# A hybrid encoder layer on one core: opening loads in order, side loads one unit ahead, up factors in every product

## The chip, the cores and the metric

One NeuronCore of a Trainium2 chip. TensorE multiplies, VectorE, ScalarE and GpSimd do elementwise work, and DMA queues that SyncE (SP) and GpSimd feed bring data from HBM to SBUF and back. The metric is the device time of one execution in microseconds. Before the change it is 2768.53 us (median of 3 runs, 2767.21 to 2771.9).

## The reference

Everything is float32; 1024 tokens, 2048 channels.

```python
mod = silu(c) @ w_ada + b_ada;  shift, scale, gate = split(mod, 3)       # w_ada: 2048 x 6144
h = rms_norm(x, g_pre) * (1 + scale) + shift
q, f, i, z, bb, cc, vb, zb = split(h @ w_in, 8)                          # w_in: 2048 x 8192
y_a = rms_norm(hgrn2(q, log f, 1 - f, i)) * silu(z)                      # 8 heads, chunks of 64 tokens
y_b = bb * causal_conv3(cc * vb) * silu(zb)
m_a, m_b = split(sigmoid(h @ w_merge + b_merge), 2)                      # w_merge: 2048 x 4096
out = (m_a * (y_a @ w_up_a) + m_b * (y_b @ w_up_b)) @ w_o                # w_up: 1024 x 2048 each
x = x + gate * rms_norm(out, g_post)
```

## The kernel before, in words

**The products.** Each large product is cut into 2x2 blocks and done with seven block products in place of eight (Strassen's scheme in Winograd's form); the stages are called p1, p6, p2, p7, p5, p4 and p3. A factor is a sum of blocks. Each float32 operand is split into a high part and a rest (`split_w` for weights, tiles w_hi and w_lo; `split_h` for activations, tiles called fp or yp), and one block product is three matmuls: hi x hi, hi x rest, rest x hi (`mm3`, L118). ScalarE casts the high part, VectorE subtracts to get the rest. A product of a unit has 24 matmuls of 128x512 (8 groups g of 3).

**The opening (L301 to L313).** x is loaded in 16 tiles, normed, and transposed on TensorE into xT. `ada_pair(q)` (L228) computes a quarter of shift and scale: 16 loads of w_ada (`ada_load`, L218; 512 KB each); the scale row is summed by TensorE into prow (L235), the shift row by VectorE into row_v, one multiply-add per load half (L239). Eight small matmuls pa (L244) turn the rows into columns a_c and sh_c. After the next pair `factors_a` makes from them the activations of two groups g and their factors for p1, p6, p2 and p7, which stay in SBUF. The scheduler orders the DMA issues on SP by its own simulated time line unless `keep_in_program_order` pins them.

**Phase 1 (L404).** 48 units: 32 of w_in (a head's or a convolution tile's two column blocks) and 16 of w_merge. `unit_a(u)` (L329) loads four weight blocks into a ring of five "raw" buffers, makes the sums s1, s2 and s4 and the difference in a21 on VectorE, and does p1, p6, p2 and p7. The sums and partial results are written to DRAM. Side work hangs on the units: `factors_b` makes the factors for p5, p4 and p3 (u below 16), `gate_step` sums the gate row of w_ada (u from 16), `sums_o` makes the block sums of w_o (u from 32). Side loads go into the shared pool `big` of 38 slots of 512 KB, and are issued with the sums that use them.

**Phase 2 (L682).** For each unit p5, p4 and p3, with the recurrence and the convolution as side steps in a list `later`. From unit 33 on, when `later` is empty, a step of `y_factors` (L634) makes the factors yp of the up-projections from the branch results y, and writes them to yf_scr in DRAM.

**The up-projections (`up`, L724).** First branch B, then A: 28 loads of 512 KB bring the factors yp back from yf_scr, then 8 units of seven products with 12 matmuls each. Gates g are loaded by GpSimd into `big` slots. After that comes the output product with w_o.

**What sets the order.** The order on each engine is fixed when the kernel is built, by the scheduler's simulated time line; a tile that is to reuse a slot waits for the slot's last reader.

Of the kernel before, what the change touches and what calls it, by code (L numbers as in the profile page):

```python
# [26 lines left out]
def tile_hgrn2_shortconv_block(  # L27
# [145 lines left out]
    ph = ph_pool.__enter__()  # L173
    xrow = [[None] * 2 for _ in range(8)]
# [26 lines left out]
    def transpose_x(hf):  # L201
        for k in range(KT):
# [6 lines left out]
            if k % 2:  # L209
# [46 lines left out]
    def factors_a(gs, vec=()):  # L256
# [26 lines left out]
        for g, b11, b12, b21, b22 in parts:  # L283
            keep_f("p7", g, b12)
# [15 lines left out]

    for si in range(8):  # L301
# [18 lines left out]
    units = [(w_in_v, (2 * j) * 1024 + i * P, (2 * j + 1) * 1024 + i * P) for i in range(NH) for j in range(4)]  # L320
    units += [(w_merge_v, 256 * m, 256 * m + P) for m in range(16)]

    def load_q(view, par, e0):
        raw = wp.tile([P, 8, P], F32, tag="raw", name="w_raw", bufs=5)
        nc.sync.dma_start(out=raw, in_=view[:, par, :, e0:e0 + P])
        return raw

    def unit_a(u):
        view, e1, e2 = units[u]  # L329
        a11, a21 = load_q(view, 0, e1), load_q(view, 0, e2)  # L330
        a22, a12 = load_q(view, 1, e2), load_q(view, 1, e1)
        o = ph.tile([P, 3, HS], F32, tag="o", name="o", bufs=2)
        s1, s2, s4 = (ph.tile([P, 8, P], F32, tag=f"s{n}", name=f"s{n}") for n in (1, 2, 4))
        px, py = ps("mm", "px"), ps("mm", "py")
        w1 = split_w(a11)
        if u:
            product(px, w1, fa["p1"])
        nc.vector.tensor_add(out=s1, in0=a21, in1=a22)
        nc.vector.tensor_sub(out=s2, in0=s1, in1=a11)
        nc.gpsimd.dma_start(out=s_scr[u][:, 0], in_=s1.rearrange("p a b -> p (a b)"))  # L340
        w6 = split_w(s2)
        if u == 0:
            for gs in (range(6), (6, 7)):
                product(px, w1, fa["p1"], pin=True, gs=gs)
                product(py, w6, fa["p6"], pin=True, gs=gs)
        nc.scalar.copy(out=o[:, 2], in_=px)
        if u:
            product(py, w6, fa["p6"])
        nc.vector.tensor_add(out=o[:, 1], in0=o[:, 2], in1=py)
        nc.vector.tensor_sub(out=s4, in0=a12, in1=s2)  # L350
        nc.gpsimd.dma_start(out=s_scr[u][:, 1], in_=s4.rearrange("p a b -> p (a b)"))
        product(px, split_w(a12), fa["p2"], more=True)
        nc.scalar.copy(out=o[:, 0], in_=px)
        nc.vector.tensor_sub(out=a21, in0=a11, in1=a21)
        product(py, split_w(a21), fa["p7"], more=True)
        nc.vector.tensor_add(out=o[:, 2], in0=o[:, 2], in1=py)
        nc.gpsimd.dma_start(out=u_scr[u], in_=o)
# [280 lines left out]
    def y_factors(br, g):  # L638
# [17 lines left out]
    side = [f for g in range(4) for br in (1, 0) for f in y_factors(br, g)]  # L656
# [37 lines left out]
    for n, (u, s) in enumerate(seq):  # L694
# [15 lines left out]
        elif u >= 33 and side:  # L710
# [273 lines left out]
```

## Time and profile before

| what | value |
|---|---|
| median of 3 runs | 2768.53 us (2767.21 to 2771.9) |
| profiled execution | 2769.2 us, span 2767.5 us |
| mean granted TensorE clock | 0.984 |
| TensorE busy | 2673.0 us (97%) |
| VectorE busy | 1716.7 us (62%) |
| ScalarE busy | 906.3 us (33%) |
| GpSimd busy | 280.0 us (10%) |
| DMA traffic | 631.30 MB, mean 228 GB/s |
| first product of unit 0 starts | 142.04 us |
| first product of phase 2 starts | 1213.65 us |
| first product of the up-projections starts | 2108.78 us |

The busy time of TensorE is modelled from the starts of pipelined matmuls, so that 97% is the share of time in which one was under way, at whatever clock. The clock stands beside it as the granted share of full speed. The time of the profiled execution exceeds its span by 1.7 us, which lie before and behind it.

### The profile page before, as it was taken

What the parts mean: (1) busy time and instruction counts of PE and PEld (TensorE: products, weight loads), DVE (VectorE), ACT (ScalarE), POOL (GpSimd) and SP (SyncE); (2) the same over time, 40 slices, a digit from 0 to 9 for tenths busy, and PEclk for the clock granted to TensorE, in tenths of its full rate; (3) what the DMA queues carried; (4) which work ended last, traced back from release to release, by engine and by line L of the source; (5) the groups of instructions that cost most, each with busy time, mean ns of one, the idle gap of its engine ahead of it and who ended that gap; (6) DMA issues with size and microseconds to landing.
All of it is one profiled execution on the core that took longest, in us unless ns stands there. A gap on an engine that the chain in (4) does not pass through costs nothing.

```text
span 2767.5 us, 31307 instructions
## 1 busy us (share of the span) xinstructions
PE 2673.0 (97%) x11851; PEld 2152.7 (78%) x11851; DVE 1716.7 (62%) x2096; ACT 906.3 (33%) x1176; POOL 280.0 (10%) x495
## 2 busy tenths in 40 slices
PE   4889999999999999999999999999998999999997
PEld 3267878888888888888888888888885787888786
DVE  6777886754554444546666666656563666765667
ACT  4433222222222222233344444435442222232333
POOL 2012111110000000010000000002111101100000
PEclk9899999999999999999999999999998999999999
DMA  9769999985556655584444444359999569773353
GB/s 361 286 201 313 345 349 364 346 292 179 179 192 179 182 175 177 174 316 137 133 130 133 138 146 138 110 178 374 360 363 407 187 213 335 235 282 99 99 178 142
DMA packets 420071, 631.30 MB, mean 228 GB/s; under 512 B 19564, under 2 KB 281808, under 8 KB 419792
## 3 DMA queue, kind: packets, MB, share of 16 engines
q1 hardware_dynamic: 358528, 394.31, 44.7%
q0 software_dynamic: 60208, 230.78, 21.7%
q10 hardware_dynamic: 1184, 4.20, 0.4%
q8 instruction: 93, 1.52, 0.2%
q14 instruction: 58, 0.48, 0.0%
HBM read 431.04 MB, written 198.18 MB: 227 GB/s over the span
## 4 chain that ended last, share of the span: by engine, by line
PE 81%; issue 8%; DMA 7%; DVE 2%; POOL 1%; ACT 1%; DVEq 0%; POOLq 0%; ACTq 0%; SPq 0%
PE po L866 10%; PE pz L119 7%; PE pz L122 7%; PE pz L123 7%; PE px L119 6%; PE px L123 6%; PE px L122 6%; PE py L123 6%; PE py L119 6%; PE py L122 6%; PE pw L119 4%; PE pw L122 4%; PE pw L123 4%; DMA yp<-yf_scr 3%; DMA ga_raw<-in_w_ada_dram 2%
## 5 line engine op out<-in xcount | busy, mean ns | idle before, releaser
L130 ACT CAST w_hi<-w_raw 128x1024 fp32r<-128x1024 f32 (+1 forms) x296 | 290.9, 983 | 1001.6 <-PE px L122 402.5
L131 DVE TENSOR_TENSOR w_lo<-w_raw,w_hi 128x1024 fp32r<-128x1024 f32 (+1 forms) x296 | 335.7, 1134 | 273.1 <-ACT w_hi L130 263.4
L123 PE MATMUL py<-fp,w_lo 128*128 128x512 f32 x768 | 301.2, 392 | 6.9 <-DVE w_lo L131 6.9
L123 PE MATMUL px<-fp,w_lo 128*128 128x512 f32 x768 | 300.9, 392 | 5.2 <-DVE w_lo L131 5.2
L119 PE MATMUL px<-fp,w_hi 128*128 128x512 f32 x768 | 301.2, 392 | 0.0
L122 PE MATMUL py<-fp,w_hi 128*128 128x512 f32 x768 | 299.5, 390 | 1.3 <-DVE fp L136 1.3
L119 PE MATMUL py<-fp,w_hi 128*128 128x512 f32 x768 | 299.8, 390 | 0.9 <-ACT w_hi L130 0.9
L122 PE MATMUL px<-fp,w_hi 128*128 128x512 f32 x768 | 300.0, 391 | 0.0
L866 PE MATMUL po<-w_hi,lt 128*128 128x512 f32 x896 | 244.2, 390 | 0.6 <-DVE og L900 0.6
L866 PEld LDWEIGHTS po<-w_hi,lt 128*128 128x128 f32 x896 | 168.1, 188 | 37.2 <-DVE og L900 2.2
L130 ACT CAST w_hi<-s 128x512 fp32r<-128x512 f32 (+1 forms) x112 | 90.1, 805 | 285.9 <-PE py L122 245.5
L123 PEld LDWEIGHTS py<-fp,w_lo 128*128 128x128 f32 x768 | 144.5, 188 | 41.5 <-DVE w_lo L131 11.2
L123 PEld LDWEIGHTS px<-fp,w_lo 128*128 128x128 f32 x768 | 144.8, 188 | 36.9 <-DVE w_lo L131 6.5
L122 PEld LDWEIGHTS py<-fp,w_hi 128*128 128x128 f32 x768 | 144.5, 188 | 32.1 <-DVE fp L136 1.7
L122 PEld LDWEIGHTS px<-fp,w_hi 128*128 128x128 f32 x768 | 145.1, 189 | 30.8 <-issue 0.5
L119 PEld LDWEIGHTS px<-fp,w_hi 128*128 128x128 f32 x768 | 144.9, 189 | 30.8 <-issue 0.7
L119 PEld LDWEIGHTS py<-fp,w_hi 128*128 128x128 f32 x768 | 144.5, 188 | 30.8 <-ACT w_hi L130 1.3
L119 PE MATMUL pz<-fp,hi 128*128 128x512 f32 x384 | 152.5, 397 | 3.0 <-DVE d L701 3.0
L122 PE MATMUL pw<-fp,w_hi 128*128 128x512 f32 x384 | 150.8, 393 | 0.0
L119 PE MATMUL pz<-fp,w_hi 128*128 128x512 f32 x384 | 150.5, 392 | 0.0
L123 PE MATMUL pz<-fp,lo 128*128 128x512 f32 x384 | 150.4, 392 | 0.0
L119 PE MATMUL pw<-fp,w_hi 128*128 128x512 f32 x384 | 150.4, 392 | 0.0
(286 smaller groups left out, 4959.4 us busy)
## 6 DMA issues: line engine op xcount, KB each, us to landing
w_raw<-in_w_in_dram SPq DMA_DIRECT2D x160, 512.0 KB, 5.2
s_scr<-s POOLq DMA_DIRECT2D x96, 512.0 KB, 6.0
s_raw<-s_scr SPq DMA_DIRECT2D x96, 512.0 KB, 4.3
w_raw<-in_w_merge_dram SPq DMA_DIRECT2D x80, 512.0 KB, 5.7
u_scr<-o POOLq DMA_DIRECT2D x48, 768.0 KB, 7.5
ada_raw<-in_w_ada_dram SPq DMA_DIRECT2D x64, 512.0 KB, 10.8
yf_scr<-yp POOLq DMA_DIRECT2D x56, 512.0 KB, 9.0
yp<-yf_scr SPq DMA_DIRECT2D x56, 512.0 KB, 12.8
```

The costliest lines, as they stand in the source:

```text
L119: mm = nc.tensor.matmul(o, ah, bh, start=first, stop=False, skip_group_check=True)
L122: nc.tensor.matmul(o, ah, bl, start=False, stop=False, skip_group_check=True)
L123: nc.tensor.matmul(o, al, bh, start=False, stop=last, skip_group_check=True)
L130: nc.scalar.copy(out=hi, in_=raw)
L131: nc.vector.tensor_sub(out=lo, in0=raw, in1=hi.bitcast(F32))
L866: nc.tensor.matmul(o, a, b[:, c], start=st, stop=sp, skip_group_check=True)
```

## The change

Six things are changed.

1. The loads of x, w_ada and the first two units' weights are pinned in program order on SP (`load`). The program puts unit 0's weights ahead of the last pair of rows. In the first three pairs all w_ada tiles lie in `big`. Small tiles move (`rows` into the raw ring, `row_p` into o0), and fewer copies of the second half's transposes go to VectorE.
2. Unit 0 is a generator: its splits and sums stand before the last pair of rows, its products behind the last factors, and it runs p1, p6 and p2 over the groups 0 to 5 first and 6 and 7 after, then p7.
3. `factors_b` is issued after the last sum of units 2, 4, ... 16. From unit 2 on the block a11 has buffers of its own (`ph`).
4. The loads of `gate_step` and `sums_o` are issued one unit ahead of the sums, pinned, from unit 10 and unit 26 on.
5. The steps of `y_factors` run first for branch A and then for B, one in every product from unit 33 on, and B's p1 factors stay in SBUF and are neither written nor read back.
6. The gates g of the up-projections have a ring of four; the pb loads are pinned.

The diff, without the parts that only move code of `unit_a`:

```diff
+    def load(o, i):
+        tc.keep_in_program_order(nc.sync.dma_start(out=o, in_=i))
...
-            nc.sync.dma_start(out=t, in_=x[si * P:(si + 1) * P, q * S:(q + 1) * S])
+            load(t, x[si * P:(si + 1) * P, q * S:(q + 1) * S])
...
-            if k % 2:
+            if k % 2 and (hf == 0 or k % 4 == 1):
                 nc.vector.tensor_copy(out=xT[k][:, halves[hf]], in_=p)
...
-        if n_ada[0] % 3:
+        if q < 3 or n_ada[0] % 4:
             raw = bigt(F32, "ada_raw").rearrange("p (k e) -> p k e", k=2)
         else:
-            raw = ph.tile([P, 2, HS], F32, tag="ada", name="ada_raw", bufs=4)
-        nc.sync.dma_start(out=raw, in_=w_ada_v[:, k:k + 2, t, q * HS:(q + 1) * HS])
+            raw = ph.tile([P, 2, HS], F32, tag="ada", name="ada_raw", bufs=2)
+        load(raw, w_ada_v[:, k:k + 2, t, q * HS:(q + 1) * HS])
...
+    def load_a(u):
+        view, e1, e2 = units[u]
+        if u > 1:
+            a11 = ph.tile([P, 8, P], F32, tag="a11", name="a11")
+            nc.sync.dma_start(out=a11, in_=view[:, 0, :, e1:e1 + P])
+        else:
+            a11 = load_q(view, 0, e1, pin=True)
+        return [a11] + [load_q(view, *a, pin=u < 2) for a in ((0, e2), (1, e2), (1, e1))]
...
+        if u == 0:
+            v.tensor_sub(out=a21, in0=a11, in1=a21)
+            w2 = split_w(a12, out_t=(ph.tile([P, 8, P], F32R, name="hi3a", bufs=1), wp.tile([P, 8, P], F32R, tag="raw", name="lo3a", bufs=5)))
+            yield
+            p2 = ps("mm", "p2")
+            for gs in (range(6), (6, 7)):
+                for p, w, f in ((px, w1, "p1"), (py, w6, "p6"), (p2, w2, "p2")):
+                    product(p, w, fa[f], pin=True, gs=gs)
...
     for q in range(1, 4):
+        if q == 3:
+            first = unit_a(0, load_a(0))
+            next(first)
         ada_pair(q)
         factors_a((2 * q - 2, 2 * q - 1))
-    factors_a((6, 7), vec=(7,))
+    with tc.issue_after(factors_a((6, 7), vec=(7,)).ins):
+        next(first, None)
...
     def gate_step(n):
...
-        nc.sync.dma_start(out=raw, in_=w_ada_v[:, 2 * kq:2 * kq + 2, 2, eb * HS:(eb + 1) * HS])
+        load(raw, w_ada_v[:, 2 * kq:2 * kq + 2, 2, eb * HS:(eb + 1) * HS])
+        yield
...
+    side = []
     for u in range(NU):
-        unit_a(u)
-        if u < 16:
-            if u % 2 == 0:
-                factors_b(u // 2)
-        elif u < 32:
-            gate_step(2 * u - 32)
-            gate_step(2 * u - 31)
-        elif u % 2 == 0:
-            sums_o((u - 32) // 2)
+        if u:
+            for _ in unit_a(u, load_a(u)):
+                pass
+
+        with tc.issue_after(last_sum[0]):
+            if u in range(2, 18, 2):
+                factors_b(u // 2 - 1)
+            for f in side:
+                next(f, None)
+        side = []
+        if 10 <= u < 26:
+            side = [gate_step(2 * u - 20), gate_step(2 * u - 19)]
+        elif u in range(26, 42, 2):
+            side = [sums_o((u - 26) // 2)]
+        for f in side:
+            next(f)
...
+                if br and s == "p1":
+                    first_y.append(t)
+                    continue
...
-    side = [f for g in range(4) for br in (1, 0) for f in y_factors(br, g)]
+    first_y = []
+    side = [f for br in (0, 1) for g in range(4) for f in y_factors(br, g)]
...
         if later:
             later.pop(0)()
-        elif u >= 33 and side:
+        if u >= 33 and side:
             side.pop(0)()
...
-        fy = {s: [pair(f"y{s}_{g}") for g in range(4)] for s in STAGES}
+        fy = {s: [pair(f"y{s}_{g}") for g in range(4)] for s in STAGES if not (y0 and s == "p1")}
+        if y0:
+            fy["p1"] = first_y
...
-                t = bigt(F32, "g")
+                t = ph.tile([P, S], F32, tag="g", name="g", bufs=4)
...
-            nc.sync.dma_start(out=t, in_=pb_scr[2 * du + j])
+            tc.keep_in_program_order(nc.sync.dma_start(out=t, in_=pb_scr[2 * du + j]))
```

**Where the instructions move.** On SP in the opening, before (x are the input tiles, ada_raw the tiles of w_ada, w_raw weight blocks):

```order
L180 DMA x_1_429<-in_x_dram 128x1024
L224 DMA ada_raw<-in_w_ada_dram 128x2x512 x4
L325 DMA w_raw<-in_w_in_dram 128x8x128 x5
L224 DMA ada_raw<-in_w_ada_dram 128x2x512 x60
L325 DMA w_raw<-in_w_in_dram 128x8x128 x21
```

And after, at the same place:

```order
L119 DMA x_1_428<-in_x_dram 128x1024
L119 DMA ada_raw<-in_w_ada_dram 128x2x512 x48
L119 DMA w_raw<-in_w_in_dram 128x8x128 x4
L119 DMA ada_raw<-in_w_ada_dram 128x2x512 x16
L119 DMA w_raw<-in_w_in_dram 128x8x128 x4
L318 DMA a_1443<-in_w_in_dram 128x8x128
```

Unit 0's weights have moved from behind the fourth load of w_ada to behind the 48th, and unit 1's stand behind all of them.

On VectorE at the end of the opening, before (row_v is the shift row, a_c and sh_c the columns made from it, s the block sums of unit 0):

```order
L239 SCALAR_TENSOR_TENSOR row_v<-ada_raw,c_act,row_v 128x512 x6
L247 TENSOR_TENSOR a_c<-pa,cols 128x4
L249 TENSOR_TENSOR sh_c<-pa,cols 128x4
L338 TENSOR_TENSOR s_1184<-w_raw 128x1024
L248 SCALAR_TENSOR_TENSOR a_c<-a_c,cols 128x4
L339 TENSOR_TENSOR s_1185<-s_1184,w_raw 128x1024
L354 TENSOR_TENSOR w_raw<-w_raw 128x1024
```

And after, from the end of the third pair of rows on:

```order
L134 TENSOR_TENSOR w_lo<-w_raw,w_hi 128x1024
L251 TENSOR_TENSOR a_c<-pa,cols 128x4
L253 TENSOR_TENSOR sh_c<-pa,cols 128x4
L252 SCALAR_TENSOR_TENSOR a_c<-a_c,cols 128x4
L336 TENSOR_TENSOR s_1025<-w_raw 128x1024
L337 TENSOR_TENSOR s_1026<-s_1025,w_raw 128x1024
L341 TENSOR_TENSOR w_raw<-w_raw 128x1024
L241 TENSOR_SCALAR row_v<-ada_raw,c_act 128x512
L134 TENSOR_TENSOR lo3a<-w_raw,hi3a 128x1024
L243 SCALAR_TENSOR_TENSOR row_v<-ada_raw,c_act,row_v 128x512
L134 TENSOR_TENSOR w_lo<-s_1026,w_hi 128x1024
```

The sums and splits of unit 0 have moved from behind the fourth pair of rows to its beginning.

On SP at the end of phase 2, before (d are partial results of units, yp the factors of branch B, called yf_scr in DRAM):

```order
L434 DMA d_14310<-u_scr_116 128x512
L436 DMA d_14309<-u_scr_116 128x1024
L728 DMA yp_0_14463<-yf_scr_0_0_329 128x1024
L728 DMA yp_1_14464<-yf_scr_0_1_330 128x1024
L728 DMA yp_2_14465<-yf_scr_0_2_331 128x1024
L733 DMA w_raw<-in_w_up_b_dram 128x4x256
L728 DMA yp_3_14466<-yf_scr_0_3_332 128x1024
L728 DMA yp_0_14467<-yf_scr_1_0_333 128x1024
```

And after:

```order
L474 DMA d_14299<-u_scr_116 128x1024
L469 DMA s_raw<-s_scr_164 128x1024
L774 DMA yp_0_14453<-yf_scr_1_0_333 128x1024
L311 DMA w_raw<-in_w_merge_dram 128x8x128
L774 DMA yp_1_14454<-yf_scr_1_1_334 128x1024
L473 DMA s_raw<-s_scr_164 128x1024
L774 DMA yp_2_14455<-yf_scr_1_2_335 128x1024
L779 DMA w_raw<-in_w_up_b_dram 128x4x256
```

The first loads of yp now stand between the loads of the last unit, and they are those of p6, since p1 is not loaded.

## Rows read from the trace of the kernel before

**Rows 1.** The page, parts 1 (busy us, share) and 4 (chain).

```profile
PE 2673.0 (97%) x11851; PEld 2152.7 (78%) x11851; DVE 1716.7 (62%) x2096; ACT 906.3 (33%) x1176; POOL 280.0 (10%) x495
...
PE 81%; issue 8%; DMA 7%; DVE 2%; POOL 1%; ACT 1%; DVEq 0%; POOLq 0%; ACTq 0%; SPq 0%
```

**Rows 2.** Windows by stage: us, busy us by engine, PEclk, DMA share, GB/s.

```profile
0.00:142.00 142.00, 96.73 (x323) 39.28 (x323) 98.18 (x177) 61.08 (x97) 16.56 (x21) 0.87 0.89 315
142.00:450.00 308.00, 293.93 (x1257) 238.40 (x1257) 246.51 (x290) 87.55 (x113) 46.20 (x86) 0.98 0.92 312
450.00:700.00 250.00, 250.00 (x1105) 207.01 (x1104) 150.57 (x138) 59.55 (x69) 34.17 (x64) 1.00 0.85 286
700.00:1213.00 513.00, 512.78 (x2258) 422.44 (x2257) 247.39 (x229) 121.66 (x141) 44.33 (x83) 1.00 0.61 187
1213.00:2075.00 862.00, 862.00 (x4101) 714.27 (x4100) 540.36 (x650) 374.59 (x426) 90.92 (x152) 1.00 0.58 200
2075.00:2155.00 80.00, 66.88 (x240) 48.74 (x239) 26.67 (x39) 18.04 (x25) 9.65 (x18) 0.83 0.99 385
```

**Rows 3.** Timeline, VectorE and TensorE: start us, us, engine, line, op.

```profile
139.03 0.75 DVE L239 SCALAR_TENSOR_TENSOR row_v<-ada_raw,c_act,row_v 128x512 f32<-128x512 f32 x1
...
142.04 0.48 PE L119 MATMUL px<-fp,w_hi 128*128 128x512 f32 x1
...
1213.65 0.39 PE L119 MATMUL pz<-fp,w_hi 128*128 128x512 f32 x1
```

**Rows 4.** Waits in the opening: us in total, times, longest us.

```profile
PE prow L235 <- DMA ada_raw<-in_w_ada_dram: 19.5, 4, 15.6
...
DVE row_v L237 <- DMA ada_raw<-in_w_ada_dram: 19.1, 2, 15.8
```

**Rows 5.** Windows of the opening, and its groups (busy us, mean ns).

```profile
60.00:65.00 5.00, 0.00 (x0) 0.00 (x0) 0.00 (x0) 0.00 (x0) 0.00 (x0) 0.57 1.05 388
85.00:90.00 5.00, 5.00 (x13) 0.97 (x12) 4.96 (x9) 2.43 (x5) 0.00 (x0) 1.00 0.24 59
110.00:115.00 5.00, 4.39 (x11) 0.76 (x10) 5.00 (x9) 3.14 (x6) 0.00 (x0) 1.00 1.05 387
...
L239 DVE SCALAR_TENSOR_TENSOR row_v<-ada_raw,c_act,row_v 128x512 f32<-128x512 f32 x60 | 44.9, 749 | 4.5 <-DMA ada_raw<-in_w_ada_dram 3.1
...
L136 DVE TENSOR_TENSOR fp<-xT,fp 128x512 fp32r<-128x512 f32 x24 | 15.2, 682 | 0.0
...
L278 DVE TENSOR_TENSOR xT<-keep,xT 128x512 f32<-128x512 f32 x6 | 4.1, 686 | 0.0
```

**Rows 6.** Waits of TensorE, 142 to 460, and the w_lo group.

```profile
PE py L123 <- DVE w_lo L131: 6.7, 4, 2.7
PE px L123 <- DVE w_lo L131: 5.2, 3, 2.2
PE py L122 <- DVE fp L136: 1.3, 1, 1.3
PE py L119 <- ACT w_hi L130: 0.9, 1, 0.9
...
L131 DVE TENSOR_TENSOR w_lo<-w_raw,w_hi 128x1024 fp32r<-128x1024 f32 x39 | 47.4, 1218 | 11.8 <-ACT w_hi L130 11.8
```

**Rows 7.** Windows at the up-projections' start; timeline of TensorE and SP.

```profile
2108.77:2154.30 45.53, 35.41 (x109) 23.27 (x107) 15.39 (x24) 7.33 (x13) 4.75 (x9) 0.74 0.97 376
2130.00:2140.00 10.00, 7.54 (x15) 4.27 (x16) 0.69 (x1) 0.00 (x0) 0.00 (x0) 0.50 1.03 400
...
2101.64 0.60 PE L119 MATMUL pz<-fp,hi 128*128 128x512 f32 x1 [2.98 <-DVE d L701]
...
2086.64 36.20 SPq L728 DMA_DIRECT2D yp<-yf_scr  x20
```

**Rows 8.** Waits of TensorE at the change of branch, and a window.

```profile
PE pz L119 <- DMA yp<-yf_scr: 2.8, 2, 2.5
...
2300.00:2310.00 10.00, 9.24 (x32) 6.17 (x32) 3.18 (x5) 1.15 (x2) 0.00 (x0) 0.84 1.02 408
```

More of the change, by code (lines that the diff above doesn't have):

```diff
@@ L75, in tile_hgrn2_shortconv_block @@
     make_identity(nc, ident)
-    rows_c = const.tile([16, P], F32, name="rows_c")
+    rows = wp.tile([P, S], F32, tag="raw", name="rows", bufs=5)
+    rows_a, rows_b, rows_c = rows[0:80, 0:P], rows[0:49, P:2 * P], rows[0:16, 2 * P:3 * P]
     nc.scalar.dma_start(out=rows_c, in_=c[0].rearrange("(n p) -> n p", p=P))
-    rows_a = const.tile([80, P], F32, name="rows_a")
-    rows_b = const.tile([49, P], F32, name="rows_b")
     b_rows = b_ada[0].rearrange("(n p) -> n p", p=P)
@@ L135, in split_h @@
         eng(out=t[:, 0], in_=raw)
-        nc.vector.tensor_sub(out=t[:, 1], in0=raw, in1=t[:, 0].bitcast(F32))
+        return nc.vector.tensor_sub(out=t[:, 1], in0=raw, in1=t[:, 0].bitcast(F32))
     STAGES = ("p1", "p6", "p2", "p7", "p5", "p4", "p3")
@@ L173, in tile_hgrn2_shortconv_block @@
     ph = ph_pool.__enter__()
+    o0 = ph.tile([P, 3, HS], F32, name="o0", bufs=1)
     xrow = [[None] * 2 for _ in range(8)]
@@ L229, in ada_pair @@
         prow = ps("aux", "prow")
-        row_p, row_v = (ph.tile([P, HS], F32, tag=t, name=t) for t in ("row_p", "row_v"))
+        row_p, row_v = o0[:, 0], ph.tile([P, HS], F32, tag="row_v", name="row_v")
         for k in range(0, KT, 2):
@@ L272, in keep_f @@
             fa[s][g] = pair(f"f{s}_{g}")
-            split_h(fa[s][g], raw, nc.scalar.copy)
+            return split_h(fa[s][g], raw, nc.scalar.copy)
         for g, b11, b12, b21, b22 in parts:
@@ L283, in factors_a @@
         for g, b11, b12, b21, b22 in parts:
-            keep_f("p7", g, b12)
+            last = keep_f("p7", g, b12)
+        return last
     def factors_b(g):
@@ L299, in factors_b, with load_q @@
             nc.gpsimd.dma_start(out=hb_scr[n][g], in_=t.rearrange("p a b -> p (a b)").bitcast(F32))
+    units = [(w_in_v, (2 * j) * 1024 + i * P, (2 * j + 1) * 1024 + i * P) for i in range(NH) for j in range(4)]
+    units += [(w_merge_v, 256 * m, 256 * m + P) for m in range(16)]
+    def load_q(view, par, e0, pin=False):
+        raw = wp.tile([P, 8, P], F32, tag="raw", name="w_raw", bufs=5)
+        (load if pin else nc.sync.dma_start)(raw, view[:, par, :, e0:e0 + P])
+        return raw
+    def load_a(u):
[6 more added lines that the diff above has]
+        return [a11] + [load_q(view, *a, pin=u < 2) for a in ((0, e2), (1, e2), (1, e1))]
@@ new lines, in tile_hgrn2_shortconv_block, with unit_a @@
+    last_sum = [None]
+    def unit_a(u, raws):
+        a11, a21, a22, a12 = raws
+        o = ph.tile([P, 3, HS], F32, tag="o", name="o", bufs=2) if u else o0
+        s1, s2 = (ph.tile([P, 8, P], F32, tag=f"s{n}", name=f"s{n}", bufs=1) for n in (1, 2))
+        s4 = ph.tile([P, 8, P], F32, tag="s4", name="s4") if u else s1
+        px, py = ps("mm", "px"), ps("mm", "py")
+        v = nc.vector
+        w1 = split_w(a11)
+        if u:
+            product(px, w1, fa["p1"])
+        v.tensor_add(out=s1, in0=a21, in1=a22)
+        v.tensor_sub(out=s2, in0=s1, in1=a11)
+        nc.gpsimd.dma_start(out=s_scr[u][:, 0], in_=s1.rearrange("p a b -> p (a b)"))
+        w6 = split_w(s2)
+        if u == 0:
[6 more added lines that the diff above has]
+                    product(p, w, fa[f], pin=True, gs=gs)
+        nc.scalar.copy(out=o[:, 2], in_=px)
+        if u:
+            product(py, w6, fa["p6"])
+        v.tensor_add(out=o[:, 1], in0=o[:, 2], in1=py)
+        v.tensor_sub(out=s4, in0=a12, in1=s2)
+        nc.gpsimd.dma_start(out=s_scr[u][:, 1], in_=s4.rearrange("p a b -> p (a b)"))
+        if u:
+            product(px, split_w(a12), fa["p2"], more=True)
+            nc.scalar.copy(out=o[:, 0], in_=px)
+        else:
+            v.tensor_add(out=o[:, 0], in0=o[:, 2], in1=p2)
+        if u:
+            v.tensor_sub(out=a21, in0=a11, in1=a21)
+        product(py, split_w(a21), fa["p7"], more=True)
+        last_sum[0] = v.tensor_add(out=o[:, 2], in0=o[:, 2], in1=py).ins
+        nc.gpsimd.dma_start(out=u_scr[u], in_=o)
@@ L318, in tile_hgrn2_shortconv_block @@
     ph = ph_pool.__enter__()
[L320 to L357, printed above, removed]
     gacc = [None]
@@ L390, in sums_o @@
         for t, par, c in ((b12, 0, 1), (b22, 1, 1), (b11, 0, 0), (b21, 1, 0)):
-            nc.sync.dma_start(out=t, in_=w_o_v[:, par, g, :, c, :])
+            load(t, w_o_v[:, par, g, :, c, :])
+        yield
         v = nc.vector
@@ L398, in sums_o @@
             nc.gpsimd.dma_start(out=t_scr[n][g], in_=t.rearrange("p a b -> p (a b)"))
+    side = []
     for u in range(NU):
-        unit_a(u)
-        if u < 16:
-            if u % 2 == 0:
-                factors_b(u // 2)
-        elif u < 32:
-            gate_step(2 * u - 32)
-            gate_step(2 * u - 31)
-        elif u % 2 == 0:
-            sums_o((u - 32) // 2)
+        if u:
+            for _ in unit_a(u, load_a(u)):
[12 more added lines that the diff above has]
+            next(f)
     ph_pool.__exit__(None, None, None)
@@ L724, in up @@
     def up(view, y0, g0, finish, ahead=None):
-        fy = {s: [pair(f"y{s}_{g}") for g in range(4)] for s in STAGES}
+        fy = {s: [pair(f"y{s}_{g}") for g in range(4)] for s in STAGES if not (y0 and s == "p1")}
+        if y0:
+            fy["p1"] = first_y
         for n, s in enumerate(STAGES):
+            if y0 and s == "p1":
+                continue
             for g in range(4):
```

## The prediction

> **What bounds the kernel now.** I read the page's first part and its chain of waits, then the span cut into stages, then in each stage the list of what the engines waited for. The page has TensorE busy for 97% of the span and 81% of the chain, with 8% issue and 7% DMA [rows 1]. The cut by stages shows where the other 3% and the slow clock are [rows 2]: from 700 to 2075 us TensorE has 0.2 us of idle time at full clock, so no edit there can gain anything. The losses are in four places: the opening (142 us, clock 0.87), the first units behind it (308 us with 293.93 busy, clock 0.98), the start of the up-projection (2075 to 2155, clock 0.83), and in its middle, around 2300, the change from branch B to branch A [rows 8]. What lies behind, the output projection, the change does not touch.
>
> I need the pace of a 128x512 matmul. Two stretches without waits give it: 250 us / 1105 = 0.2262 us and 513 / 2258 = 0.2272 us [rows 2]; I take 0.2267. (The 390 ns of the profile's groups are modelled ends and overlap.)
>
> All sums are against the profiled run, 2769.2 us, of which 2767.5 are span; that is 0.7 us above the median of 2768.53.
>
> **Part 1, the opening.** The first product of unit 0 starts at 142.04 [rows 3]. Behind the last VectorE sum of the last row (139.03 + 0.75) stand the pa matmuls, and the product starts 2.26 us after that sum ends; this tail stays. What makes the sum late is the loads: TensorE's prow waits 19.5 us in four pieces for ada_raw, the longest 15.6, and VectorE's first product of a row 19.1 us [rows 4]. The stages show a stretch at 60 us with no engine busy and the DMA at 388 GB/s, and one at 85 us with VectorE full and the DMA at 59 GB/s [rows 5]: the loads come in an order in which neither side keeps the other fed. Five w_raw loads stand after the fourth ada_raw, and those of unit 0 are held in the ring from then on. In the new order 48 ada_raw follow x, four w_raw, then the last 16.
>
> Two bounds hold the new opening. The DMA: 16 + 64 + 4 loads of 0.524 MB are 44.0 MB; at the 387 GB/s of rows 5, 113.8 us, with the first 20 us of x at a lower rate (some 3 us, estimated from the 315 GB/s mean of the opening, [rows 2]) 117 us. The last load is then followed by two sums (2 x 0.75) and the tail of 2.26: 121 us. VectorE: a pair of rows costs 16 x 0.749 = 12.0 us, its factors 8 x 0.682 + 4 x 0.686 = 8.2 us [rows 5], together 20 us. The first pair can end at about 52 us (x and 16 ada_raw are 32 loads, 16.8 MB, 43.4 us, + 3, + the sums still open), the next two at 73 and 94, and the fourth carries besides the sums and splits of unit 0 that are moved ahead of it: six operations of the size of w_lo, 1.22 us [rows 6], 7.3 us. 94 + 7.3 + 20 + 2.26 = 124 us. So VectorE binds, just behind the DMA; I take 124, a gain of 18.0. Bounds: 121 at the best (21.0); if the three quarters that VectorE is kept busy today in the opening stay (98.18 of 142 is 0.69, [rows 2]) about 132 (10.0). Where the six moved operations stood, their going counts in part 2; where they go, their 7.3 us are in this sum.
>
> On this the Trainium skill speaks against the change: "DMA: Bandwidth & Descriptors", section Specifications, gives about 358 GB/s as the limit of HBM for a core. By it the 44.0 MB would take 123 us and the first product would start at 130, a gain of 12 in place of 18. The trace does not agree: 387 and 388 GB/s stand over whole stretches [rows 5], so the measured rate is used.
>
> **Part 2, the units behind it.** From 142.04 to the first pz at 1213.65 [rows 3] 1071.6 us pass; 48 units x 4 products x 24 matmuls = 4608 at 0.2267 are 1044.6. The loss is 27: 14.1 us of waits (6.7 + 5.2 for w_lo, 1.3 for a factor, 0.9 for w_hi, [rows 6]), 6.2 of half clock (308 x 0.02, [rows 2]), and the gates' own pg matmuls and the like, which stay. VectorE was behind there: 246.5 of 308 us busy, with four w_lo and four sums of 1.22 us and two adds in each unit of 21.8 us, beside the second set of factors (p5, p4, p3), which the scheduler pressed into the first units. Now those come one group per two units, the sums of unit 0 are done, unit 0 has 54 matmuls (12.2 us) of three products before the last factors are needed, and VectorE's part of them is 4 + 4 + 6 operations at 0.68 us for 512 columns, 9.5 us from the a_c at its start: covered, by 2.7 us. One wait I expect to be left: in the new order the add of unit 0's last product stands ahead of unit 1's first w_lo on VectorE, 0.68 + 1.22, so 2 us. I take 3 us of waits and 1.5 of slow clock left: 14.1 + 6.2 - 4.5 = 15.8, rounded to 15. Bounds 6 (the waits halve, the clock stays) and 19.
>
> The loads for the side work are now issued one unit ahead and pinned in SP's order among the weights. From 700 to 2075 they stood there too and cost 0.2 us [rows 2], so I take zero; the rival below prices it.
>
> **Part 3, the start of the up-projection.** From 2108.77 to 2154.30 there are 109 matmuls in 45.5 us at a mean clock of 0.74; at 0.2267 they need 24.7, so 20.8 are lost, and 2.98 more just before, in a wait of p3 for a sum [rows 7]. What it waits for there is yp<-yf_scr: 20 loads issued from 2086.64 over 36.2 us, with the DMA full (400 GB/s, share 1.03) and the clock granted at 0.50 from 2130 to 2140, the lower of its two levels (1.2 and 2.4 GHz), behind the waits [rows 7]. Volume decides. The change takes out of this queue four loads (p1 stays in SBUF) and four writes, and moves six of ten gate loads behind: 14 x 0.524 = 7.3 MB, 18 us at 400 GB/s. And the factors are ready some 100 us earlier (24 steps in every product from unit 33, not in two of three to unit 44), so that the yp6 loads stand between the loads of unit 47, well before 2083. What is late next is the last yp3 group, needed about 14 us (60 of 84 matmuls) into the first unit. I take 7 of the 20.8 as left, 3 of them waits and 4 clock, and the 2.98 as gone: 16.8, say 17. Bounds 5 and 23.
>
> **Part 4, the change of branch and the denser side work.** Around 2300 the same wait costs 2.8 us, and 10 us at a clock of 0.84 another 1.6 [rows 8]. The gates' own ring frees six slots for these loads, and eight of them go ahead of the weights: 3 of 4.4 gained; bounds 0 and 4.4. In units 33 to 41 a step stands beside every product; in 1213 to 2075 VectorE is 63% and ScalarE 43% busy [rows 2], and a step (three factors: 3 x 0.68 and one or two more) fits beside 1.22 + 0.68 in 5.4 us. Zero; if ScalarE's two sigmoids and a step do meet in nine products at 1 us each, a loss of 9.
>
> **Sum.** 18 + 15 + 17 + 3 = 53; 2769.2 - 53 = 2716.2. Since terms taken singly tend to leave a rest between them, I put 2718. Its own range, by some half of the bounds' distance on each term, is 2704 to 2734.
>
> **Rivals.**
> 1. The opening stays with its old rhythm and VectorE's row of work only moves: first product at 132, and of part 2 only 6. Gain 10 + 6 + 17 + 3 = 36, 2733 us. For it: VectorE is at its bound by my sum, and the moved sums weigh on it. Against: the idle piece of 15.6 us is the order of the loads alone [rows 4].
> 2. The up-projection's start stays bound by the DMA: 24 loads are left, most waiting for the slots of branch two's factors. Gain there 5 and none at the change of branch: 18 + 15 + 5 = 38, 2731 us. For it: a DMA share of 1.03 in the stretch that waits [rows 7]. Against: the volume above.
> 3. Slower: SP takes its queue in order, and a pinned ga_raw or wo whose slot is still held by a gate's sum (or wo by its store) stops the weights behind it. Place: units 10 to 41, most of which carry such loads. A late w_lo costs up to 2.7 us at a time [rows 6]; at 2.2 us in each unit 32 x 2.2 = 70 us: 2769.2 - 53 + 70 = 2786. It decides from 53 / 32 = 1.7 us per unit. Against it: the same loads stand in units 16 to 47 of before, and from unit 26 or so on TensorE is full [rows 2].
> 4. It does not do what it says in time: the freed opening is given back as waits of the first units (loads of unit 1 stand after all rows), and the up-projection as in rival 2: 2769.2 - 5, within the noise to 2764.
>
> Chances: forecast 0.66, first 0.13, second 0.13, third 0.05, fourth 0.03. A range from 2700 to 2745 takes in the forecast with its bounds and the first two rivals. A measurement of this kernel tells 0.2% (5.5 us) from no change: faster 0.93, same 0.03, slower 0.04.
>
> **What the new profile would show.** The first px at 121 to 127 with no stretch of idle DMA before it; a DMA rate of 380 or more from 20 to 110 us; w_lo waits of 3 us or less behind it; first pz at 1180 to 1184; at the start of the up-projection under 8 us of loss and a clock above 0.85. The forecast is wrong if prow still waits over 6 us, if waits appear in units 10 to 41, or if yp loads still land after their products.

## The result and the profile after

The changed kernel takes 2905.01 us (median of 4 runs, 2900.25 to 2911.12) against 2768.26; the ratio is 1.0499, with a 95% interval of 1.0478 to 1.052. It is 137 us slower, where 50 us less was forecast. The profiled run took 2900.25 us, span 2898.5.

The first product of each stage gives this table (us). The forecast puts the 2.98 us wait of part 3 in phase 2, where it stands, and part 4 in the up-projections:

| stage | before | after | difference | forecast |
|---|---|---|---|---|
| opening, to the first product | 142.0 | 131.3 | -10.7 | -18 |
| phase 1, to the first pz | 1071.6 | 1205.8 | +134.2 | -15 |
| phase 2, to the first up product | 895.1 | 915.0 | +19.8 | -3 |
| up-projections, to the first po | 335.2 | 315.4 | -19.8 | -17 |
| output product | 323.5 | 331.0 | +7.5 | 0 |

A line of the page of after, to be read beside [rows 1]: TensorE's matmuls are the same 11851, and its share of the span falls from 97% to 94%. (The chain of after goes back only to 1069.9 us, so its shares can't be read beside those of before.)

```profile
PE 2715.3 (94%) x11851; PEld 2176.0 (75%) x11851; DVE 1710.6 (59%) x2093; ACT 907.9 (31%) x1179; POOL 278.0 (10%) x491
```

The windows of after, cut at its own stages (columns as in [rows 2]); the last answers to the first window of [rows 7]:

```profile
0.00:131.30 131.30, 92.35 (x324) 38.08 (x324) 102.44 (x178) 64.82 (x103) 16.07 (x22) 0.92 0.98 349
131.30:405.00 273.70, 259.30 (x1098) 209.23 (x1099) 154.21 (x167) 72.60 (x92) 25.53 (x48) 0.98 0.61 192
405.00:700.00 295.00, 274.17 (x1164) 221.85 (x1163) 175.29 (x196) 67.47 (x81) 30.00 (x56) 0.98 0.74 235
700.00:1337.10 637.10, 570.89 (x2359) 458.92 (x2359) 303.19 (x292) 126.71 (x148) 68.32 (x128) 0.95 0.70 221
1337.10:2000.00 662.90, 662.90 (x3223) 549.59 (x3222) 421.29 (x495) 284.38 (x318) 54.15 (x80) 1.00 0.46 149
2000.00:2170.00 170.00, 154.75 (x642) 126.13 (x641) 101.59 (x138) 73.07 (x93) 33.97 (x64) 0.94 0.98 369
2170.00:2252.00 82.00, 82.00 (x363) 67.90 (x362) 29.65 (x34) 27.44 (x27) 5.86 (x11) 1.00 0.83 287
2252.00:2297.50 45.50, 40.43 (x164) 29.26 (x163) 23.46 (x37) 9.68 (x16) 3.74 (x7) 1.00 0.99 386
```

The first 45.5 us of the up-projections hold 164 matmuls in place of 109: that part came as forecast. TensorE has idle pieces all through phase 1: 14.4 + 20.8 + 66.2 = 101 us in the three windows, and some 43 us more at the lower clock (637 x 0.05 + 569 x 0.02, estimated from their mean clocks). On the mean of these windows neither VectorE nor the DMA is full. What TensorE waited for over the whole run (us in total, times, longest), to be read beside [rows 6]:

```profile
PE py L126 <- DVE w_lo L134: 58.3, 32, 6.9
PE px L126 <- DVE w_lo L134: 37.9, 16, 5.3
PE pz L122 <- DVE d L743: 15.2, 4, 4.8
...
PE po L912 <- ACT lt L138: 6.0, 1, 6.0
```

And what VectorE waited for in phase 1 of after; `a` is the block a11, which from unit 2 on has a buffer of its own:

```profile
DVE w_raw L360 <- DMA a<-in_w_in_dram: 134.1, 23, 8.7
DVE s L337 <- DMA a<-in_w_merge_dram: 66.4, 7, 10.1
DVE s L336 <- DMA w_raw<-in_w_merge_dram: 65.1, 12, 9.2
DVE w_raw L360 <- DMA a<-in_w_merge_dram: 64.8, 9, 7.6
```

One turn of it, from the timelines of VectorE, ScalarE, SP and TensorE of after (start us, us):

```profile
197.12 1.22 DVE L134 TENSOR_TENSOR w_lo<-a,w_hi 128x1024 fp32r<-128x1024 f32 x1
206.67 1.23 DVE L360 TENSOR_TENSOR w_raw<-a,w_raw 128x1024 f32<-128x1024 f32 x1 [8.33 <-DMA a<-in_w_in_dram]
...
209.61 1.22 DVE L134 TENSOR_TENSOR w_lo<-s,w_hi 128x1024 fp32r<-128x1024 f32 x1
...
202.37 1.05 ACT L133 CAST w_hi<-s 128x1024 fp32r<-128x1024 f32 x1 [4.88 <-PE py L125]
...
198.36 0.37 SPq L318 DMA_DIRECT2D a<-in_w_in_dram  x1
...
210.88 0.50 PE L126 MATMUL py<-fp,w_lo 128*128 128x512 f32 x1 [2.43 <-DVE w_lo L134]
```

The w_lo of this unit's a11 is its buffer's last reader and ends at 198.3. SP issues the next unit's a11 at 198.36, into the same buffer. The next thing in VectorE's queue is L360, the difference a21 of the next unit, which needs just that load: VectorE stands 8.33 us. Behind it stands the w_lo of s2 of this unit, for which TensorE waits with p6; its w_hi had been made by 203.4.

### The profile page after: what moved, and what is told of

It is laid out like the page before. It is cut to its first block, busy times and chain, and to the rows that moved or that the text cites. A ratio compares the mean times of both kernels' runs of the same rounds, so it can differ in the third digit from the quotient of the medians.

```text
span 2898.5 us, 31235 instructions
## 1 busy us (share of the span) xinstructions
PE 2715.3 (94%) x11851; PEld 2176.0 (75%) x11851; DVE 1710.6 (59%) x2093; ACT 907.9 (31%) x1179; POOL 278.0 (10%) x491
## 4 chain that ended last, share of the span: by engine, by line
PE 53%; DMA 5%; DVE 3%; issue 1%; ACT 0%; DVEq 0%; SPq 0%; ACTq 0%
PE po L912 10%; PE pz L122 7%; PE pz L126 7%; PE pz L125 7%; PE pw L125 3%; PE pw L122 3%; PE pw L126 3%; DMA a<-in_w_merge_dram 2%; PE py L126 2%; PE px L126 2%; PE py L122 2%; PE px L122 2%; PE py L125 2%; PE px L125 2%; DMA w_raw<-in_w_merge_dram 2%
## 5 line engine op out<-in xcount | busy, mean ns | idle before, releaser
L133 ACT CAST w_hi<-w_raw 128x1024 fp32r<-128x1024 f32 (+1 forms) x249 | 241.1, 968 | 856.5 <-PE py L125 243.4
L126 PE MATMUL py<-fp,w_lo 128*128 128x512 f32 x768 | 314.0, 409 | 58.4 <-DVE w_lo L134 58.3
L134 DVE TENSOR_TENSOR w_lo<-w_raw,w_hi 128x1024 fp32r<-128x1024 f32 (+1 forms) x249 | 278.0, 1116 | 127.6 <-ACT w_hi L133 125.2
L122 PE MATMUL py<-fp,w_hi 128*128 128x512 f32 x768 | 309.6, 403 | 4.9 <-DVE o L351 4.8
L125 PE MATMUL py<-fp,w_hi 128*128 128x512 f32 x768 | 308.3, 401 | 0.0
L126 PEld LDWEIGHTS py<-fp,w_lo 128*128 128x128 f32 x768 | 150.6, 196 | 104.6 <-DVE w_lo L134 73.4
L122 PEld LDWEIGHTS py<-fp,w_hi 128*128 128x128 f32 x768 | 150.4, 196 | 37.5 <-issue 6.3
L125 PEld LDWEIGHTS py<-fp,w_hi 128*128 128x128 f32 x768 | 150.4, 196 | 32.9
L360 DVE TENSOR_TENSOR w_raw<-a,w_raw 128x1024 f32<-128x1024 f32 x46 | 56.2, 1223 | 198.9 <-DMA a<-in_w_in_dram 134.1
L122 PE MATMUL pz<-fp,hi 128*128 128x512 f32 x384 | 155.6, 405 | 15.2 <-DVE d L743 15.2
L125 PE MATMUL pz<-fp,hi 128*128 128x512 f32 x384 | 153.0, 399 | 0.0
L125 PE MATMUL pw<-fp,w_hi 128*128 128x512 f32 x384 | 150.8, 393 | 0.0
## 6 DMA issues: line engine op xcount, KB each, us to landing
ada_raw<-in_w_ada_dram SPq DMA_DIRECT2D x64, 512.0 KB, 10.4
```

The source lines that it names most:

```text
L133: nc.scalar.copy(out=hi, in_=raw)
L134: nc.vector.tensor_sub(out=lo, in0=raw, in1=hi.bitcast(F32))
L360: v.tensor_sub(out=a21, in0=a11, in1=a21)
```

## The experiments

Three runs below (e2, e3, e9) were made once; the repeated runs of the changed kernel lie 11 us apart, and what is read from the three is larger. Two theories stood at the start. A: a11's one buffer, with VectorE's queue as above. B: the side loads pinned in SP's queue (my third rival). For phase 2 a third, C: the step in every product asks for more than the DMA gives.

**a11 in the ring** (label e1)

```diff
-        if u > 1:
-            a11 = ph.tile([P, 8, P], F32, tag="a11", name="a11")
-            nc.sync.dma_start(out=a11, in_=view[:, 0, :, e1:e1 + P])
-        else:
-            a11 = load_q(view, 0, e1, pin=True)
+        a11 = load_q(view, 0, e1, pin=u < 2)
```

> The changed kernel, but the block a11 of every unit comes through the raw ring of five again; everything else stays. Theory A (one buffer for a11): its load for the next unit can only be issued behind the w_lo of this unit's a11, and VectorE then stands in its queue before the difference a21 of the next unit (L360), with this unit's w_lo of s2 behind it. Then phase 1 falls from 1206 us to 1075 or less and the time from 2905 to 2770 to 2780. Theory B (side loads pinned in SP's queue, my third rival): only units 2 to 9, which have no side loads, recover, some 17 us, and the time is 2880 or more.

2781.33 us (ratio to before 1.0044, 1.003 to 1.0059). Phase 1 falls by 122.7 us, to 1083.1; the other stages are within 2.5 us of after. That is theory A, a little short of its size (1075 or less, 2770 to 2780).

**Side loads not pinned** (e2)

```diff
-        load(raw, w_ada_v[:, 2 * kq:2 * kq + 2, 2, eb * HS:(eb + 1) * HS])
+        nc.sync.dma_start(out=raw, in_=w_ada_v[:, 2 * kq:2 * kq + 2, 2, eb * HS:(eb + 1) * HS])
```

and the same in `sums_o`.

> The changed kernel, but the loads of the gate steps and of the block sums of w_o are not pinned in SP's order; a11 keeps its one buffer. Theory A (a11's one buffer): 2890 us or more, with the waits for w_lo as they are. Theory B (pinned side loads): the waits from unit 10 on go, 2820 us or less.

2918.87 us (one run), phase 1 1220.9. Theory B falls, as far as the pin goes. But SP stands before these loads without the pin too (in phase 1 113.2 us for the stores of wo; 94.0 in after), so e2 alone does not price that standing. The trace of after does: of 27 weight loads that stand right behind a side load that waited, 24 had to wait for their own slot even after it, and the other three were held up by 5.0 us together.

**a11's buffer alone, in the kernel before** (e3)

```diff
-        a11, a21 = load_q(view, 0, e1), load_q(view, 0, e2)
+        if u > 1:
+            a11 = ph.tile([P, 8, P], F32, tag="a11", name="a11")
+            nc.sync.dma_start(out=a11, in_=view[:, 0, :, e1:e1 + P])
+        else:
+            a11 = load_q(view, 0, e1)
+        a21 = load_q(view, 0, e2)
```

> The kernel before, with one part of the change alone: from unit 2 on a11 has one buffer of its own in place of the raw ring. Theory A: slower by 60 us or more, 2830 to 2900, with VectorE waiting for a11 at the difference a21. Theory B: 2768 within 6 us.

2841.15 us (one run): phase 1 1146.7, 75 more than before. One part of the change suffices for more than half of the loss in phase 1.

**VectorE's order** (e9)

```diff
+        before6, split_w.six = getattr(split_w, "six", None), split_w.last
...
+        with tc.issue_after(before6.ins):
             v.tensor_sub(out=a21, in0=a11, in1=a21)
```

> The changed kernel with a11's one buffer, but VectorE's order is set so that the difference a21 of a unit always stands behind the w_lo of s2 of the unit before; nothing else is altered. If the place in VectorE's queue is what makes a late a11 costly, as theory A says, phase 1 falls from 1206 us, to some 1150 (the w_lo of a12 still stands behind it). If it is only that p1 of the next unit itself gets its a11 late, phase 1 stays at 1200 to 1210.

2832.77 us (one run), phase 1 1138.7: 67 us of the 123 go with the place of this one difference in the queue. VectorE's waits of e9 in phase 1; the wait of the difference for a11 from w_in is down from 134.1 to 21.6, the one for the later blocks is not:

```profile
DVE s L337 <- DMA a<-in_w_merge_dram: 67.4, 7, 11.3
...
DVE w_raw L362 <- DMA a<-in_w_in_dram: 21.6, 18, 3.2
```

What is left is in good part a place in the queue again, as the expectation had it: s2 of the next unit (L337) needs the late a11 too, and behind it stands the w_lo of a12, for which TensorE waits with p2. Ten such waits make some 32 us. One of them (its w_hi had been cast by 1104.5):

```profile
1109.79 1.22 DVE L337 TENSOR_TENSOR s<-s,a 128x1024 f32<-128x1024 f32 x1 [9.69 <-DMA a<-in_w_merge_dram]
...
1113.20 1.22 DVE L134 TENSOR_TENSOR w_lo<-w_raw,w_hi 128x1024 fp32r<-128x1024 f32 x1
...
1114.47 0.80 PE L126 MATMUL px<-fp,w_lo 128*128 128x512 f32 x1 [4.99 <-DVE w_lo L134]
```

**Steps in two of three products** (e4, on top of e1)

```diff
-        if u >= 33 and side:
+        elif u >= 33 and side:
```

> As the run with a11 in the ring, and besides the steps of the up factors stand in two of three products again (only where no recurrence step is due). Theory C: the step in every product asks for 423 GB/s in units 33 to 41 (6.9 MB in 16.3 us), above the 390 to 410 that the DMA gives, so weights land late there; that is the 20 us which phase 2 lost. Then phase 2 falls from 915 to 895 to 898 us and the time is 10 to 20 us below the run with a11 in the ring alone. Theory D (phase 2 loses because d is read back late, in the new order of SP at the end of phase 2): no change against that run, within 5 us.

2766.1 us (ratio 0.9984, 0.9973 to 0.9995). Phase 2 884.8, the up-projections 328.8: together 1213.6 against 1232.9 in e1 and 1230.4 before. So the step in every product costs 19.3 us, the size that theory C gave, and theory D falls. (The expectation's 895 to 898 for phase 2 alone was not met: in e4 the first up product stands ahead of the last p3 of phase 2, which moves 24 matmuls, 5.4 us, into the next stage, and TensorE has no wait left in phase 2.) One window over the last merge units, first of e1, then of e4:

```profile
1900.00:2080.00 180.00, 161.25 (x675) 131.59 (x674) 96.33 (x129) 72.32 (x89) 29.80 (x57) 0.93 0.95 349
```

```profile
1900.00:2080.00 180.00, 180.00 (x796) 149.05 (x795) 107.99 (x140) 82.07 (x99) 32.66 (x63) 1.00 0.97 355
```

With fewer steps a product nearly the same DMA rate serves 796 matmuls in place of 675. In e1 the DMA runs at 409 GB/s just before TensorE falls behind, and a merge weight takes 17.2 us to land from 1900 to 1980, against 12.8 in e4:

```profile
1920.00:1940.00 20.00, 20.00 (x90) 16.58 (x89) 9.24 (x12) 6.89 (x8) 2.66 (x5) 1.00 1.04 409
1940.00:1960.00 20.00, 20.00 (x89) 16.55 (x89) 11.88 (x17) 9.93 (x13) 4.24 (x8) 1.00 1.01 367
1960.00:1980.00 20.00, 15.22 (x56) 12.04 (x55) 11.71 (x18) 7.51 (x10) 4.25 (x8) 0.83 1.02 388
...
w_raw<-in_w_merge_dram SPq DMA_DIRECT2D x4, 512.0 KB, 17.2
```

That the DMA is what TensorE waited for is not shown, though. All four waits of after in phase 2, 15.2 us, end with the sum d on VectorE, and in front of it stand operations of the steps. The longest, in after:

```profile
2082.64 0.69 DVE L139 TENSOR_TENSOR yp<-y,yp 128x512 fp32r<-128x512 f32 x1
...
2088.31 0.68 DVE L165 TENSOR_TENSOR y<-t,y 128x512 f32<-128x512 f32 x1
2088.91 1.22 DVE L134 TENSOR_TENSOR w_lo<-w_raw,w_hi 128x1024 fp32r<-128x1024 f32 x1
2090.05 0.68 DVE L743 TENSOR_TENSOR d<-d,pz 128x512 f32<-128x512 f32 x1
...
2090.78 0.80 PE L122 MATMUL pz<-fp,hi 128*128 128x512 f32 x1 [4.78 <-DVE d L743]
```

From 2082.64 to 2088.91 VectorE works without a gap through ten operations of the steps, then comes a w_lo, and only then d, whose last load had landed at 2086.49. TensorE waits from 2086.0. So the late load makes at most 0.5 us of this wait; the rest is order on VectorE. In e1 the same ten operations stand ahead of d before waits of 4.8 and 9.1 us. e4 takes away bytes and operations at once, and no run separates them.

**The rest of phase 1 and the output product** (e5 to e8, e10 to e14). e5 is e4 with the side loop of before (loads with their sums, not pinned, not held) and the pb loads unpinned:

```diff
-        with tc.issue_after(last_sum[0]):
-            if u in range(2, 18, 2):
-                factors_b(u // 2 - 1)
-            for f in side:
-                next(f, None)
...
+        if u < 16:
+            if u % 2 == 0:
+                factors_b(u // 2)
+        elif u < 32:
+            side = [gate_step(2 * u - 32), gate_step(2 * u - 31)]
+        elif u % 2 == 0:
+            side = [sums_o((u - 32) // 2)]
         for f in side:
             next(f)
+            next(f, None)
```

> The run with a11 in the ring and steps in two of three products, with two further parts undone: the side work of phase 1 stands where it stood before (factors from unit 0, gate steps from 16, sums of w_o from 32, loads issued with their sums and not pinned), and the loads of pb are not pinned. Theory E (the look-ahead and its place behind the last sum put side sums between a late s1 and a waiting w_lo): phase 1 falls from 1086 to 1072 or less. Theory F (the opening hands its late weights on to the first units, whatever the side work): phase 1 stays at 1080 to 1090. With the stage behind the up-projections back from 333 to 324: about 2743 us by E, 2757 by F.

2757.34 us (ratio 0.9945, 0.993 to 0.996): phase 1 1077.2 against 1085.9. Between E and F.

e6 is e4 with the pb loads alone unpinned:

> The run with a11 in the ring and steps in two of three products, and besides the pb loads of the last branch unpinned. If the pinning holds back the last pb, and by it m and the lt casts of the output product: the stage behind the up-projections falls from 333 to 324 us and the time from 2766 to 2757. If it is the gates' ring of four that delays the last merge: no change, 2766 within 4.

2768.46 us (0.999, 0.998 to 0.9999), the last stage 333.0: the pin is not it.

e7 is the kernel before with the up part alone:

> The kernel before with the up part alone: branch A's factors first, B's p1 factors kept in SBUF, gates in a ring of four (to make room, the small rows of the opening lie in the raw ring); steps in two of three products as before. Phase 2 and the up-projections together fall from 1230 to 1214 us as in the run with two of three: 2752 us, or 2761 if the 9 us behind the up-projections come from the ring of four.

2765.52 us (0.9976, 0.9966 to 0.9985): 1215.2 for phase 2 and the up-projections, but 332.9 behind them. 15 us won, 9 lost; nearer to the expectation's 2761 than to its 2752.

e8 is the kernel before with the opening alone:

> The kernel before with the opening alone: loads in order, unit 0's sums ahead of the last rows, three products over the first six groups; side loop, a11 and the up part as before. The first product at 131 in place of 142. By theory E phase 1 at 1072 or less: 2757 us or below. By theory F phase 1 at 1080 to 1090: 2768 us, the 10.7 us of the opening all given back.

2765.28 us (0.9977, 0.9968 to 0.9986): first product at 131.6, phase 1 1079.3. Of 10.4 us won, 7.7 are given back by these profiles, and 5 if phase 1 is taken from e7 or e10, whose phase 1 has the code of before (1074.3 and 1074.2). The medians are 6.1 us apart. So theory F, by which all of it goes, is met only in part.

e10 is the kernel before with the gates' ring of four alone:

```diff
-                t = bigt(F32, "g")
+                t = ph.tile([P, S], F32, tag="g", name="g", bufs=4)
```

> The kernel before with the gates' ring of four alone (and the opening's small rows in the raw ring, to make room). If the ring is what delays the last merge, its m and the lt casts: the stage behind the up-projections is 333 us in place of 323.5, phase 2 and the up-projections together 1230 or somewhat less: 2773 to 2779. If not: 2769 within 4.

2767.11 us (0.9999, 0.9987 to 1.001), the last stage 331.3, the up-projections 328.6: the ring makes both differences, +7.8 and -6.6, and is worth nothing. Its wait of the output product, as in after, where before had none:

```profile
PE po L865 <- ACT lt L134: 6.2, 1, 6.2
```

e11 is e5 with the gates in the shared slots again:

> The run with the old side loop, a11 in the ring, steps in two of three and pb unpinned, and besides the gates in the shared slots as before. The stage behind the up-projections returns from 330 to 324, the up-projections lose a little of their 16.3 us gain (ten gate loads early again): 2750 us, against 2757 with the ring of four.

2758.46 us (0.9977, 0.9967 to 0.9986): last stage 323.7, the up-projections 341.3. The expectation of 2750 missed by 8, for the loads of the gates come back at their start.

e12 is e11 with the second factors in units 2, 4, ... 16, not held:

> As the run with the gates in the shared slots, and the second set of factors begins at unit 2 in place of unit 0. The wait of unit 1's first product for its w_hi (5.3 us at the hand-over with the old side loop, 1.5 with the new one) should fall, and phase 1 with it from 1077 to about 1071: 2744 us. If that wait is only the late load of unit 1's weights: the same time as that run, within 4.

2758.81 us (0.9972, 0.9962 to 0.9981), and the wait of 5.3 us at unit 1 is still there. The scheduler had moved the factors forward into unit 0 again, so that this run tells nothing of them. e13 puts them there and holds them; the lines that differ from e12:

```diff
         if u in range(2, 18, 2):
+            with tc.issue_after(last_sum[0]):
                 factors_b(u // 2 - 1)
```

The rest of e13 is e5.

> The run with the old side loop (ring of four for the gates, pb unpinned), and the second set of factors held behind the last sum of units 2, 4, ... 16, as in the change; gate steps and sums of w_o as before the change. In the run with the factors from two the scheduler had pulled them forward into unit 0 again, in front of unit 1's w_hi on ScalarE. If that order is what costs the 5.3 us at the hand-over: phase 1 falls from 1077 to 1068 to 1072 and the time from 2757 to 2750. If holding factors behind a sum is what makes the repeated w_lo waits of the look-ahead runs: phase 1 rises to 1080 or more, 2760.

2757.3 us (0.9954, 0.9941 to 0.9967). Phase 1 is 1072.8, 4.4 below e5, and the 5.3 us are gone; the median does not show it, and e11, whose phase 1 has the code of e5, has 1074.1, so that 3 of the 4.4 us are within what two profiles differ by. e14 is the counterpart, factors as before and only the look-ahead of the gate steps and sums of w_o:

> The counterpart: the second set of factors as before the change (from unit 0, not held), the gate steps and the sums of w_o one unit ahead and held behind the last sum, as in the change; a11 in the ring, steps in two of three, pb unpinned. If the look-ahead of these loads makes the w_lo waits of units 10 to 41 (some 17 us of waits there): phase 1 stays at 1083 or more, and the time at 2763 or more. If not: phase 1 1077, 2757.

2771.6 us (1.0007, 0.9996 to 1.0018), phase 1 1097.2. So the look-ahead of the side work (earlier, pinned, and held behind the last sum, which this run does not separate) is what costs, and the held factors are not. TensorE's waits for w_lo in phase 1, first of e13, then of e14:

```profile
PE py L126 <- DVE w_lo L134: 6.2, 13, 1.5
```

```profile
PE py L126 <- DVE w_lo L134: 17.8, 20, 2.9
```

The longest of these waits in e14:

```profile
1003.61 1.23 DVE L332 TENSOR_TENSOR s<-w_raw 128x1024 f32<-128x1024 f32 x1 [6.85 <-DMA w_raw<-in_w_merge_dram]
...
1005.35 1.22 DVE L419 TENSOR_TENSOR wo<-wo 128x1024 f32<-128x1024 f32 x1
...
1007.62 1.22 DVE L134 TENSOR_TENSOR w_lo<-s,w_hi 128x1024 fp32r<-128x1024 f32 x1
...
1008.89 0.79 PE L126 MATMUL py<-fp,w_lo 128*128 128x512 f32 x1 [2.93 <-DVE w_lo L134]
```

The sum s1 (L332) of the next unit waits for its load, and a sum of w_o (L419) stands between it and the w_lo that TensorE waits for. In all but one of this run's waits on the w_lo of s2 from unit 10 on, a side sum stands there.

## Why the prediction was wrong

**The failed step** is in part 2, "I take 3 us of waits and 1.5 of slow clock left". It priced what leaves phase 1 and not what the change adds there. That a11 gets a buffer of its own stands in the change as its third item, and has no term in the sum: I took it for more room, while it takes a11 out of a ring with a spare slot and puts it where the next load must wait for the last reader of this one. The order of VectorE, with the next unit's L360 ahead of this unit's w_lo of s2, could be read before the run. 122.7 us of the 134.2 go with it (e1), and 75 come with it alone (e3); the 48 between are what it costs only together with the rest of the change, and were not taken apart. On VectorE's queue the Trainium skill says the same ("TensorE: Matmul & The Clock Gate", Part 1, on queue depths): ScalarE and VectorE are strict FIFO. The trace agrees: 8.33 us in front of L360, with a w_lo behind it whose w_hi had been made by 203.4. I had that rule for SP alone.

**The third rival** had the sign and part of the place, at half the price (70 us, where phase 1 came out 149 us above the forecast), but not the mechanism: without the pin the loss is the same (e2), and weights behind a waiting side load were held by it for 5.0 us in all. The waits also begin before unit 10, where there are no such loads. The forecast's sentence that the side loads cost zero failed too, by another road: their sums, held behind the last sum of a unit and not spread by the scheduler, come between a late s1 and a waiting w_lo. e14 against e5, one run's profile each, is 20 us of phase 1; the medians are 14 apart (the profiled run of e14 is 7 above its median).

**The opening** failed in one term. The periods were right: a_c of the second, third and fourth pair comes 21.5, 21.4 and 27.6 us after the one before; 21, 21 and 20 + 7.3 stood in the sum. The first pair ends at 61, not 52:

```profile
60.91 0.16 DVE L251 TENSOR_TENSOR a_c<-pa,cols 128x4 f32<-128x4 f32 x1 [4.43 <-PE pa L248]
...
82.41 0.16 DVE L251 TENSOR_TENSOR a_c<-pa,cols 128x4 f32<-128x4 f32 x1 [0.78 <-PE pa L248]
...
103.85 0.16 DVE L251 TENSOR_TENSOR a_c<-pa,cols 128x4 f32<-128x4 f32 x1 [0.82 <-PE pa L248]
...
131.47 0.16 DVE L251 TENSOR_TENSOR a_c<-pa,cols 128x4 f32<-128x4 f32 x1 [1.96 <-PE pa L248]
```

The loads were not what held it: the 32nd had landed at 48.0 us. TensorE's row sums (prow) and VectorE's 16 sums of the first pair stand behind the transposes of x and their copies, which I let run beside the loads; and four prow of the next pair stand between the two sets of pa:

```profile
47.63 8.74 PE L239 MATMUL prow<-ada_raw,c_act 128*1 128x512 f32 x20
57.04 1.05 PE L248 MATMUL pa<-ones,o 1*128 1x1 f32 x8 [0.66 <-ACT o L244]
58.02 1.88 PE L239 MATMUL prow<-ada_raw,c_act 128*1 128x512 f32 x4
59.82 1.05 PE L248 MATMUL pa<-ones,row_v 128*128 128x1 f32 x8
```

That 131.3 is near the 132 of the first rival is luck: the old rhythm is gone (prow waits 3.5 us for its loads, where it waited 19.5). From 60 to 80 us the DMA moved 384 GB/s. The 358 GB/s of the Trainium skill ("DMA: Bandwidth & Descriptors", Specifications) did not show as a limit.

**Phase 2** failed at "Zero; if ScalarE's two sigmoids and a step do meet": the step in every product costs some 19 us (e4). I had counted a step as three operations and one or two more that fit in 5.4 us, and not asked where they stand: ten of them, 6.3 us, stood one behind the other on VectorE ahead of the sum d. That is the same fault as with a11, the order on VectorE. The DMA was full besides: by my estimate the units that make the factors ask for 6.9 MB in 16.3 us, 423 GB/s, and for 356 with steps in two of three products, near the 355 of e4. How much of the 19 us the late loads make was not separated; in the one wait shown it is at most 0.5 of 4.8.

**The start of the up-projections** was right: 164 matmuls in 45.5 us leave 8.3 of the 20.8 us (7 forecast), and the stage, with the change of branch, is 19.8 us shorter (17 forecast). But 6.6 of that is the ring of four (e10), and this is paid back at the output product, where the last merge comes late. "What lies behind, the output projection, the change does not touch" was wrong by 7.5 us; the sum had no term for it.

**What beats both kernels**, by half a per cent: e5 and e13 are 0.55% and 0.46% below the kernel before (their intervals overlap): the new opening, a11 in the ring, the old side loop (in e13 with the factors held), and the up part with steps in two of three products. Open is why the opening's gain of 8.6 us or so stays only in part in the runs without the look-ahead, apart from the 5.3 us at unit 1; and the share of clock and wait in e3 that is not in VectorE's order was not taken apart.

## What to carry to other kernels

When a tile moves from a ring to one buffer of its own, write down the turn: last reader, issue, landing, first reader; then look at what stands behind that first reader in its engine's queue. Before side work is made denser or moved, look where its operations will stand in the queue of the engine that makes the next sum, and add up the bytes that a unit asks for. And read the order of the changed program for every buffer that it renames, not only for the edits that promise something.

## What the runs showed that I had not expected

In one stretch short waits came with about half again as much loss by the clock: from 700 to 1337 us TensorE is idle for 66 us in pieces of 7 us or less, and the mean granted clock is 0.95, which is 32 us more by estimate. And the mean DMA share of a stage (0.61 to 0.74 in phase 1 of after) tells little of how long one load takes there: a11 took 3.9 to 15.6 us, 7.4 in the median; while these loads were under way the share was 0.83 in the median:

```profile
DMA to landing us min/median/max: 3.9/7.4/15.6
```
